# Two-bank PSUM tiles for attention scores and accumulators, and the two heads' score products issued in turn

## The chip, the cores and the metric

The kernel runs on one core of one Trainium2 chip. The core has a matrix engine (TensorE, PE in the profile) with its weight loads (PEld), VectorE (DVE), ScalarE (ACT), GpSimd (POOL) and SyncE (SP), which issues the transfers. PE writes its products to PSUM, here eight banks of 512 fp32 numbers for each of 128 partitions, and DVE and ACT read them from there. The metric is the device time of one execution in microseconds (us); less is better.

## The reference

Two layers of a decoder trunk on 256 tokens of width 1024, all in fp32. Each layer is a half SwiGLU feed-forward block (FFN, width 2816), a token mixer, and a second half FFN. Each block is normalised before and after.

```python
x = x + 0.5 * rms_norm(swiglu(rms_norm(x, g[0]), ...), g[1])
h = rms_norm(x, g[2])
m = pool_mixer(h, ...)  if i % 2 == 0 else  nsa_mixer(h, ...)
x = x + rms_norm(m, g[3])
x = x + 0.5 * rms_norm(swiglu(rms_norm(x, g[4]), ...), g[5])
```

The mixer of layer 0 pools: for each of four channel groups the mean over the last 2, 4, 8 or 16 tokens less the token itself, then a 256x256 product, a bias and a scale. The mixer of layer 1 is sparse attention with 16 heads of 64 numbers, 4 heads to a key group, and three branches: compressed blocks, selected blocks and a window. With 256 tokens the selected and the window branch each see all earlier tokens, so each is a causal softmax over the same mask but with keys and values of its own:

```python
s = jnp.einsum('bqgrd,btgd->bgrqt', qb, kb) * scale
p = jax.nn.softmax(jnp.where(mask, s, NEG_INF), axis=-1)
return jnp.einsum('bgrqt,btgd->bqgrd', p, vb)
```

## The kernel before

The tokens are two row tiles (t = 0, 1) of 128. An fp32 product is three matmuls on operands split into a high and a low part (mm3, L304 to L306; split and pieces_of make the parts, high on ACT, low on DVE, L294, L295, L309, L310). Weights arrive in pieces from HBM all through the program. The order of the instructions on each engine isn't written out: a scheduler, which simulates a timeline, chooses it, and Tile, the layer below, allots buffers from pools and puts in the waits. Both see a tile as one thing.

PSUM is two pools of four banks. psG holds short-lived products (tiles named g). psA has four one-bank tiles named acc, and acc_tiles hands out two of them, one for each half of 512 columns. These are the accumulators of an FFN's down products for a row tile (down), of the pooling stage's group product (pool_gemm) and its pooled output (pooled), of the attention output, and the score tiles of attention.

An accumulated pair goes through finish, which calls post: rstd squares both halves on ACT (L336, tile junk, with the sum into ssq), DVE adds the sums (L339, ms), POOL takes the power -0.5 (L341, rs), DVE multiplies each half by a gain (L348, into fx) and adds it to x (L350). For the next block emit then scales the row (L356, L357, L393) and transposes it on PE (L364, tile g). In the pooling stage group copies the two halves of the group product to pyh (ACT, L589) and pyl (DVE, L590), and pooled multiplies them by band matrices (L602).

Attention scores are made by qk(t, g). For each of two head pairs (pr) it fills one unit: two heads (par = 0, 1), whose queries and keys stand on partitions 0 to 63 and 64 to 127. Each head's scores for both branches are 256 columns for t = 0 and 512 for t = 1: three products (L837, operands kT and q), one product that adds the mask (L839, identr with amaskr), a maximum on DVE (L841, tile ast), and an exponential with its sum for each branch on ACT (L843, to fx or big). With two row tiles, four groups and two pairs there are 16 units, 8 of 256 and 8 of 512 columns, between 666 and 737 us. Later pv transposes the weights on PE (L881), splits them (PTh on ACT, PTl on DVE), and multiplies by the values (L862). The loop in qk is written so that the heads' products follow each other by twos, but each head has a tile of its own, and the scheduler is free to take one head's four products before the other's.

Of the kernel before, what the change touches and what calls it, by code (L numbers as in the profile page):

```python
# [9 lines left out]
F32 = mybir.dt.float32  # L10
# [5 lines left out]
PSUM = bass.MemoryType.PSUM  # L16

P = 128
# [218 lines left out]
def _trunk(ctx: ExitStack, tc: tile.TileContext, d, out):  # L237
    nc = tc.nc
    pp = ctx.enter_context(tc.tile_pool(name="pp", bufs=1))
    wp = ctx.enter_context(tc.tile_pool(name="wp", bufs=3))  # L240
    psA = ctx.enter_context(tc.tile_pool(name="psA", bufs=4, space=PSUM))
    psG = ctx.enter_context(tc.tile_pool(name="psG", bufs=4, space=PSUM))

    x = [pp.tile([P, DM], F32, name=f"x{t}") for t in range(NT)]
# [77 lines left out]
        return [v[:, H[h]] for h in range(2)]  # L322

    def acc_tiles():
        r = []
        for _ in range(2):
            acc = psA.tile([P, 512], F32, name="acc")
            r.append(acc)
        return r

    def rstd(src, half, t):
        s = pp.tile([P, 2], F32, name=f"ssq{t}", bufs=2)
# [76 lines left out]
    def ffn(i, j, pre, g_post, nxt, W0, preload, me=None):  # L409
        wg, wu, wd = d[f"wg{i}{j}"], d[f"wu{i}{j}"], d[f"wd{i}{j}"]  # L410
        with tc.tile_pool(name="fp", bufs=2, reuse_waits="tile") as fp:
# [8 lines left out]
            with ExitStack() if first else after(pre.h[0]):  # L420
                U = [W0[2], ksplit(piece(wu[:, 2048:4096], fp, "d", ND, 512), 8)]
            acc = [acc_tiles() for t in range(NT)]
            A = lambda t, k: [q[:, k, t * P:(t + 1) * P] for q in xT]
            hT, WD = {}, {}
# [146 lines left out]
    def pool_gemm(t, pre, W):  # L571
        acc = acc_tiles()
        xT = pre.at(t)
        for g in range(4):
            for k in range(2):
                m = mm3(acc[g // 2][:, g % 2 * 256:(g % 2 + 1) * 256], [q[:, 2 * g + k, :] for q in xT], W[2 * g + k], k == 0, k == 1)
        return acc, m

    def pool_mixer(pre, g_post, nxt, W0, preload, prep):
        with tc.tile_pool(name="mp", bufs=1, reuse_waits="tile") as mp:  # L580
# [12 lines left out]
            def pooled(t):  # L593
                o = acc_tiles()
                for g in range(4):
                    sl = slice(g * 256, (g + 1) * 256)
                    mm = [(sel[:, g, :], bias[q]) for q in range(2)]
                    mm += [(band[:, (t + b) * 4 + g, :], ys[b][q][:, sl]) for b in range(t + 1) for q in range(2)]
                    if t == 0:
                        mm.append((blo[:, g, :], ys[0][0][:, sl]))  # L600
                    for n, (A, B) in enumerate(mm):
                        nc.tensor.matmul(o[g // 2][:, g % 2 * 256:(g % 2 + 1) * 256], A, B, start=n == 0, stop=n == len(mm) - 1)  # L602
                return o
# [28 lines left out]
    def nsa(pre, g_post, nxt, W0, preload):  # L632
        with tc.tile_pool(name="np", bufs=1, reuse_waits="tile") as np_:
            identr = np_.tile([P, P], F32R, name="identr")
            amaskr = np_.tile([P, P], F32R, name="amaskr")
# [180 lines left out]
            def qk(t, g):  # L816
                nk = P * (t + 1)
                q = qT[g // 2, t]
                PP[t, g] = []
                for pr in range(2):  # L820
                    st = np_.tile([P, 2, 4], F32, name="ast", bufs=4)
                    pk_ = 2 * (g % 2) + pr
                    if pr == 0:
                        pe = fx[g % 2]
                    else:
                        pe = np_.tile([P, DM], F32, name="big", bufs=2)
                    pe = pe.rearrange("p (a k) -> p a k", a=4)
                    os_, mm = [], []
                    for par in range(2):
                        sp = psA.tile([P, 512], F32, name="acc")  # L830
                        o = sp[:, :2 * nk].rearrange("p (b k) -> p b k", b=2)
                        rs = slice(par * 64, (par + 1) * 64)
                        os_.append(o)
                        mm.append(([v[rs, pk_, :] for v in q], [v[rs, g, :, :nk] for v in kT]))
                    for i, j in ((0, 0), (0, 1), (1, 0)):
                        for o, (A, B) in zip(os_, mm):
                            nc.tensor.matmul(o, A[i], B[j], start=i + j == 0, stop=False)  # L837
                    for par, o in enumerate(os_):
                        nc.tensor.matmul(o[:, :, nk - P:], identr, amaskr[:, None, :].to_broadcast([P, 2, P]), start=False, stop=True)  # L839
                        i = par * 2  # L840
                        nc.vector.tensor_reduce(st[:, 0, i:i + 2], o, axis=AX.X, op=OP.max, negate=True)  # L841
                        for b in range(2):
                            nc.scalar.activation(pe[:, par * 2 + b, :nk], o[:, b, :], AF.Exp, bias=st[:, 0, i + b:i + b + 1],  # L843
                                                 accum_out=st[:, 1, i + b:i + b + 1])
                    yield
                    PP[t, g].append(pe)
                    r = np_.tile([P, 4], F32, name="ar", bufs=4)
                    nc.vector.reciprocal(r, st[:, 1])
                    gv = gates[t][:, 16:48].rearrange("p (b h) -> p h b", b=2)[:, 4 * g + 2 * pr:4 * g + 2 * pr + 2, :]
                    rv = r.rearrange("p (a b) -> p a b", b=2)  # L850
                    nc.vector.tensor_mul(rv, rv, gv)
                    nc.gpsimd.tensor_tensor(pe[:, :, :nk], pe[:, :, :nk], r[:, :, None].to_broadcast([P, 4, nk]), op=OP.mult)
                    yield
# [63 lines left out]
            qs, qn, ec, hm, wc, wo, acc = {}, {}, {}, {}, {}, [], []  # L917
# [17 lines left out]
            def step(kind, i, j):  # L935
                if kind in ("qk", "pv"):
                    if (kind, i, j) not in gens:
                        gens[kind, i, j] = {"qk": qk, "pv": pv}[kind](i, j)
# [57 lines left out]
    for c, hs, ls in ((0, [], pre[0].s), (1, [], pre[0].s), (2, pre[0].h[0], pre[0].h[0]), (3, pre[0].h[0], pre[0].h[0])):  # L996
        v = [q[:, c * 512:(c + 1) * 512] for q in W[0]]
        r = raw[c // 2][:, c % 2 * 512:(c % 2 + 1) * 512]
# [29 lines left out]
```

## Time and profile before

| | |
|---|---|
| median of 3 runs | 962.27 us (962.24 to 967.14) |
| profiled execution, span from first to last instruction | 963.9 us |
| mean granted PE clock | 0.993 of full speed |
| PE busy | 947.9 us, 98% |
| DVE, ACT, POOL busy | 581.1, 473.1, 82.2 us |

The profile is one execution; of its time only the span is recorded, and what lies around it is not. All times of rows are counted from the span's start. A row of a timeline gives the start, the busy time, engine, line, operation, written tile and read tiles with their shapes (partitions x elements), and how many like instructions it joins; in brackets stands the idle time before it and what ended it. PE's matmuls overlap, so their busy times add up to more than the time that passes: the price of a group is read from its start to the start of the next work.

### The profile page before, as it was taken

The page shows a single profiled execution, that of the slowest core. Times are in us where ns is not written, and L with a number is a line of the kernel's source. Part 1 is how long each engine was busy: PE and PEld are TensorE (multiplying, and loading weights), DVE is VectorE, ACT ScalarE, POOL GpSimd, SP SyncE. Part 2 cuts the span into 40 slices and gives each one's busy share as a digit, 9 for nine tenths or more (in the row PEclk, how much of TensorE's full clock was granted, in tenths as well). Part 3 has the DMA queues.
Part 4 walks back from the last instruction along what each step waited for, and adds up shares of the span by engine and source line. Part 5 has one row for each costly group of instructions (what it writes and reads, how often), then busy time and mean ns, then how long its engine had stood idle before and what let it go on. Part 6 is the DMA issues. An engine that isn't in the chain of part 4 may idle for free.

```text
span 963.9 us, 15935 instructions
## 1 busy us (share of the span) xinstructions
PE 947.9 (98%) x6418; PEld 861.8 (89%) x6418; DVE 581.1 (60%) x833; ACT 473.1 (49%) x812; POOL 82.2 (9%) x78
## 2 busy tenths in 40 slices
PE   8999999999999999999999999999999999999997
PEld 6999999989999999899999998888677799999996
DVE  5755554586854555567554456677986867554532
ACT  6744444355644444446443443545765655444421
POOL 1000000231000000120000001001455110000000
PEclk9999999999999999999999999999999899999999
DMA  8866666334866656248655652672200358666511
GB/s 302 280 219 235 209 190 191 101 129 136 291 230 201 191 176 218 89 144 293 216 180 186 203 177 68 256 260 90 88 1 5 122 194 295 203 197 180 184 45 44
DMA packets 47467, 169.14 MB, mean 175 GB/s; under 512 B 5529, under 2 KB 6041, under 8 KB 46882
## 3 DMA queue, kind: packets, MB, share of 16 engines
q1 hardware_dynamic: 47394, 168.13, 53.5%
q8 instruction: 50, 0.82, 0.4%
q14 instruction: 23, 0.19, 0.1%
HBM read 167.06 MB, written 1.05 MB: 174 GB/s over the span
## 4 chain that ended last, share of the span: by engine, by line
PE 91%; DVE 4%; ACT 2%; DMA 1%; issue 1%; POOL 1%; SPq 0%; DVEq 0%; POOLq 0%; ACTq 0%
PE g L306 18%; PE g L305 18%; PE g L304 18%; PE acc L306 9%; PE acc L304 9%; PE acc L305 9%; PE g L457 2%; PE acc L837 1%; PE g L862 1%; DVE wlo L295 1%; PE g L881 1%; PE g L364 1%; PE acc L602 1%; PE acc L839 1%; ACT whi L294 1%
## 5 line engine op out<-in xcount | busy, mean ns | idle before, releaser
L306 PE MATMUL g<-xTh,wlo 128*128 128x256 f32 x1152 | 327.8, 285 | 0.0
L305 PE MATMUL g<-xTl,whi 128*128 128x256 f32 x1152 | 326.8, 284 | 0.0
L304 PE MATMUL g<-xTh,whi 128*128 128x256 f32 x1152 | 324.5, 282 | 0.0
L295 DVE TENSOR_TENSOR wlo<-raw,whi 128x1024 fp32r<-128x1024 f32 (+2 forms) x252 | 244.4, 1012 | 94.0 <-ACT whi L294 93.4
L294 ACT ACTIVATE whi<-raw 128x1024 fp32r<-128x1024 f32 (+2 forms) x252 | 204.5, 862 | 184.2 <-issue 67.2
L304 PEld LDWEIGHTS g<-xTh,whi 128*128 128x128 f32 x1152 | 218.5, 190 | 1.2
L305 PEld LDWEIGHTS g<-xTl,whi 128*128 128x128 f32 x1152 | 216.7, 188 | 1.2
L306 PEld LDWEIGHTS g<-xTh,wlo 128*128 128x128 f32 x1152 | 217.6, 189 | 0.0
L295 DVE TENSOR_TENSOR dlo<-raw,dhi 128x1024 fp32r<-128x1024 f32 (+1 forms) x128 | 119.4, 956 | 120.0 <-ACT dhi L294 119.6
L294 ACT ACTIVATE dhi<-raw 128x1024 fp32r<-128x1024 f32 (+1 forms) x128 | 104.3, 843 | 143.3 <-DMA raw<-in_wd 137.0
L305 PE MATMUL acc<-dlo,hTh 128*128 128x512 f32 x288 | 112.6, 391 | 0.0
L304 PE MATMUL acc<-dhi,hTh 128*128 128x512 f32 x288 | 112.4, 390 | 0.0
L306 PE MATMUL acc<-dhi,hTl 128*128 128x512 f32 x288 | 112.1, 391 | 0.0
L429 DVE TENSOR_TENSOR sg<-sg,g 128x512 f32<-128x512 f32 x44 | 30.1, 685 | 92.3 <-PE g L306 92.3
L304 PE MATMUL g<-whi,xTh 128*128 128x256 f32 (+2 forms) x240 | 76.7, 322 | 1.9 <-ACT xTh L309 1.0
L306 PE MATMUL g<-whi,xTl 128*128 128x256 f32 (+2 forms) x240 | 76.6, 321 | 0.2
L305 PE MATMUL g<-wlo,xTh 128*128 128x256 f32 (+2 forms) x240 | 76.1, 319 | 0.0
L341 POOL TENSOR_TENSOR rs<-ms,neghalf 128x1 f32<-128x1 f32 x24 | 13.2, 548 | 611.5 <-DVE ms L339 611.5
L306 PEld LDWEIGHTS acc<-dhi,hTl 128*128 128x128 f32 x288 | 54.0, 188 | 11.5
L305 PEld LDWEIGHTS acc<-dlo,hTh 128*128 128x128 f32 x288 | 54.1, 188 | 10.6
L304 PEld LDWEIGHTS acc<-dhi,hTh 128*128 128x128 f32 x288 | 54.2, 188 | 10.4
L304 PEld LDWEIGHTS g<-whi,xTh 128*128 128x128 f32 x240 | 46.5, 194 | 5.7 <-ACT xTh L309 2.2
(194 smaller groups left out, 1137.5 us busy)
## 6 DMA issues: line engine op xcount, KB each, us to landing
raw<-in_wu SPq DMA_DIRECT2D x88, 512.0 KB, 4.6
raw<-in_wd SPq DMA_DIRECT2D x88, 512.0 KB, 4.6
raw<-in_wg SPq DMA_DIRECT2D x86, 512.0 KB, 4.2
raw<-in_win SPq DMA_DIRECT2D x18, 512.0 KB, 4.0
gain<-in_gains SPq DMA_DIRECT2D x11, 512.0 KB, 3.7
raw<-in_wo SPq DMA_DIRECT2D x8, 512.0 KB, 4.5
raw<-in_win SPq DMA_DIRECT2D x4, 304.0 KB, 2.9
raw<-in_wg SPq DMA_DIRECT2D x4, 256.0 KB, 4.6
```

What stands on the lines that cost most here:

```text
L294: nc.scalar.activation(hi[:, n + a:n + b], r[:, a:b], AF.Copy)
L295: nc.vector.tensor_tensor(lo[:, n + a:n + b], r[:, a:b], hi[:, n + a:n + b].bitcast(F32), op=OP.subtract)
L304: nc.tensor.matmul(o, A[0], B[0], start=start, stop=False)
L305: nc.tensor.matmul(o, A[0], B[1], start=False, stop=False)
L306: return nc.tensor.matmul(o, A[1], B[0], start=False, stop=stop)
L341: nc.gpsimd.tensor_tensor(r, v, neghalf, op=OP.pow)
L364: i = nc.tensor.transpose(pt[:, k, :], src[:, (4 * h + k) * P:(4 * h + k + 1) * P], ident)
L429: nc.vector.tensor_mul(sg, sg, pu)
L457: nc.tensor.matmul(o[:, u * 256:(u + 1) * 256], A(t, k)[i], B[u][k][j], start=n == 0, stop=n == len(its) - 1, skip_group_check=True)
L602: nc.tensor.matmul(o[g // 2][:, g % 2 * 256:(g % 2 + 1) * 256], A, B, start=n == 0, stop=n == len(mm) - 1)
L837: nc.tensor.matmul(o, A[i], B[j], start=i + j == 0, stop=False)
L839: nc.tensor.matmul(o[:, :, nk - P:], identr, amaskr[:, None, :].to_broadcast([P, 2, P]), start=False, stop=True)
```

## The change

psA has two tiles of two banks each instead of four of one bank: the same memory. acc_tiles returns the two halves of one such tile. In qk a unit takes its two score banks from one acc_tiles call, and the two mask products are issued behind all six score products, ahead of the maxima.

```diff
--- before.py
+++ after.py
@@ -238,7 +238,7 @@
     nc = tc.nc
     pp = ctx.enter_context(tc.tile_pool(name="pp", bufs=1))
     wp = ctx.enter_context(tc.tile_pool(name="wp", bufs=3))
-    psA = ctx.enter_context(tc.tile_pool(name="psA", bufs=4, space=PSUM))
+    psA = ctx.enter_context(tc.tile_pool(name="psA", bufs=2, space=PSUM))
     psG = ctx.enter_context(tc.tile_pool(name="psG", bufs=4, space=PSUM))
 
     x = [pp.tile([P, DM], F32, name=f"x{t}") for t in range(NT)]
@@ -322,11 +322,8 @@
         return [v[:, H[h]] for h in range(2)]
 
     def acc_tiles():
-        r = []
-        for _ in range(2):
-            acc = psA.tile([P, 512], F32, name="acc")
-            r.append(acc)
-        return r
+        acc = psA.tile([P, 2, 512], F32, name="acc")
+        return [acc[:, h] for h in range(2)]
 
     def rstd(src, half, t):
         s = pp.tile([P, 2], F32, name=f"ssq{t}", bufs=2)
@@ -826,17 +823,18 @@
                         pe = np_.tile([P, DM], F32, name="big", bufs=2)
                     pe = pe.rearrange("p (a k) -> p a k", a=4)
                     os_, mm = [], []
+                    sp = acc_tiles()
                     for par in range(2):
-                        sp = psA.tile([P, 512], F32, name="acc")
-                        o = sp[:, :2 * nk].rearrange("p (b k) -> p b k", b=2)
+                        o = sp[par][:, :2 * nk].rearrange("p (b k) -> p b k", b=2)
                         rs = slice(par * 64, (par + 1) * 64)
                         os_.append(o)
                         mm.append(([v[rs, pk_, :] for v in q], [v[rs, g, :, :nk] for v in kT]))
                     for i, j in ((0, 0), (0, 1), (1, 0)):
                         for o, (A, B) in zip(os_, mm):
                             nc.tensor.matmul(o, A[i], B[j], start=i + j == 0, stop=False)
+                    for o in os_:
+                        nc.tensor.matmul(o[:, :, nk - P:], identr, amaskr[:, None, :].to_broadcast([P, 2, P]), start=False, stop=True)
                     for par, o in enumerate(os_):
-                        nc.tensor.matmul(o[:, :, nk - P:], identr, amaskr[:, None, :].to_broadcast([P, 2, P]), start=False, stop=True)
                         i = par * 2
                         nc.vector.tensor_reduce(st[:, 0, i:i + 2], o, axis=AX.X, op=OP.max, negate=True)
                         for b in range(2):
```

Line numbers of the changed kernel are three lower behind acc_tiles (L837 is L834, L839 is L836 and L841 is L839 there, L843 is L841, L348 is L345).

On PE, where the third unit of 512 columns is multiplied (tiles acc, keys kT, queries q, transposes of fx by csm), there stands in the order of before:

```order
L862 MATMUL g_6917<-PTh_6918,VC0_6076 128x512 [waits Pool_49]
L862 MATMUL g_6917<-PTl_6919,VC0_6076 128x512 [waits Pool_49]
L837 MATMUL acc_7053<-kTh_6062,qh01_6765 128x512 [waits DVE_49,Activation_49]
L837 MATMUL acc_7053<-kTl_6063,qh01_6765 128x512
L837 MATMUL acc_7053<-kTh_6062,ql01_6766 128x512
L839 MATMUL acc_7053<-amaskr_6059,identr_6058 128x2x128
L837 MATMUL acc_7054<-kTh_6062,qh01_6765 128x512 [waits DVE_49,Activation_49]
L837 MATMUL acc_7054<-kTl_6063,qh01_6765 128x512
L837 MATMUL acc_7054<-kTh_6062,ql01_6766 128x512
L839 MATMUL acc_7054<-amaskr_6059,identr_6058 128x2x128
L881 MATMUL g_6928<-csm_74,fx0_69 128x128 [waits Activation_49,Pool_49]
```

and in that of after:

```order
L879 MATMUL g_6913<-csm_74,fx0_69 128x128 [waits DVE_49,Pool_49]
L879 MATMUL g_6913<-csm_74,fx0_69 128x128
L879 MATMUL g_6924<-csm_74,fx0_69 128x128 [waits Activation_49]
L879 MATMUL g_6924<-csm_74,fx0_69 128x128
L834 MATMUL acc_6959<-kTh_6051,qh01_6754 128x512 [waits DVE_49,Activation_49]
L834 MATMUL acc_6959<-kTh_6051,qh01_6754 128x512
L834 MATMUL acc_6959<-kTl_6052,qh01_6754 128x512 x2
L834 MATMUL acc_6959<-kTh_6051,ql01_6755 128x512 x2
L836 MATMUL acc_6959<-amaskr_6048,identr_6047 128x2x128 x2
L787 MATMUL g_6943<-kbd_6064,y_6822 128x32 [waits DVE_49]
L787 MATMUL g_6943<-kbd_6064,y_6822 128x32 x3
```

The two heads' products, one head whole after the other before, are now by twos in one tile, and two transposes each of the tiles behind have moved ahead of them. Only the unit's first product carries a wait in the new order.

On DVE, in the middle of the scores, with the maxima of two small units (ast from acc), there stands before:

```order
L841 TENSOR_REDUCE ast_7218<-acc_7219 128x2 [waits PE_49]
L851 TENSOR_TENSOR ar_7123<-ar_7123,gates1_6061 128x4 [waits DVE_49]
L841 TENSOR_REDUCE ast_7218<-acc_7220 128x2 [waits PE_49]
L310 TENSOR_TENSOR VC1_6077<-g_7026,VC1_6077 128x64 [waits Activation_49]
L310 TENSOR_TENSOR xTh_6950<-of_6952,xTh_6950 128x256 [waits Activation_49]
L841 TENSOR_REDUCE ast_7264<-acc_7266 128x2 [waits PE_49]
L848 RECIPROCAL ar_7188<-ast_7170 128x4 [waits Activation_49]
L899 TENSOR_TENSOR of_7020<-g_6990,y_7019 64x256 [waits DVE_49,Activation_49]
L899 TENSOR_TENSOR of_7020<-g_6990,y_7019 64x256
L851 TENSOR_TENSOR ar_7188<-ar_7188,gates1_6061 128x4 [waits DVE_49]
L310 TENSOR_TENSOR Pcl_7044<-g_7041,Pch_7043 128x128 [waits Activation_49]
L841 TENSOR_REDUCE ast_7264<-acc_7267 128x2 [waits PE_49]
```

and after, where the same two units are acc_7200 and acc_7246 (the first maximum of acc_7200 stands eight rows further up):

```order
L839 TENSOR_REDUCE ast_7244<-acc_7246 128x2 [waits PE_49]
L310 TENSOR_TENSOR PTl_7073<-g_7067,PTh_7072 128x512 [waits Activation_49,Pool_49]
L839 TENSOR_REDUCE ast_7199<-acc_7200 128x2 [waits Activation_49]
L310 TENSOR_TENSOR PTl_7084<-g_7078,PTh_7083 128x512 [waits PE_49,Activation_49]
L839 TENSOR_REDUCE ast_7244<-acc_7246 128x2 [waits Activation_49]
L310 TENSOR_TENSOR PTl_7115<-g_7109,PTh_7114 128x512 [waits PE_49,Activation_49]
L846 RECIPROCAL ar_7229<-ast_7199 128x4 [waits Activation_49]
```

Each maximum waited for PE; now the second of a unit waits for ACT. The second maximum of the first of these units stands behind the first maximum of the next one.

On DVE at the end of the kernel, where the first row tile of the last FFN is finished, there stands before:

```order
L348 TENSOR_TENSOR fx0_69<-acc_7897,gain_8026 128x512 [waits Activation_49]
L339 TENSOR_SCALAR ms0_9624<-ssq0_9619 128x1 [waits Activation_49]
L348 TENSOR_TENSOR fx0_69<-acc_7898,gain_8026 128x512
L350 SCALAR_TENSOR_TENSOR x0_67<-fx0_69,rs0_9626,x0_67 128x512 [waits Pool_49]
L350 SCALAR_TENSOR_TENSOR x0_67<-fx0_69,rs0_9626,x0_67 128x512 [waits DVE_49]
```

and after, from one row ahead:

```order
L310 TENSOR_TENSOR hTl_9561<-sg_9557,hTh_9560 128x512 [waits Activation_49]
L336 TENSOR_SCALAR ms0_9593<-ssq0_9588 128x1 [waits Activation_49]
L345 TENSOR_TENSOR fx0_69<-acc_7868,gain_7995 128x512 x2
L347 SCALAR_TENSOR_TENSOR x0_67<-fx0_69,rs0_9595,x0_67 128x512 [waits DVE_49,Pool_49]
L347 SCALAR_TENSOR_TENSOR x0_67<-fx0_69,rs0_9595,x0_67 128x512 [waits DVE_49]
```

The multiplication of half 0 stood ahead of ms and now stands behind it, with that of half 1.

## Rows read from the trace of the kernel before

**Rows 1.** The page: engines' busy time, share, instructions; chain that ended last, by engine.
```profile
PE 947.9 (98%) x6418; PEld 861.8 (89%) x6418; DVE 581.1 (60%) x833; ACT 473.1 (49%) x812; POOL 82.2 (9%) x78
...
PE 91%; DVE 4%; ACT 2%; DMA 1%; issue 1%; POOL 1%; SPq 0%; DVEq 0%; POOLq 0%; ACTq 0%
```

**Rows 2.** Windows: length, then busy us (instructions) of PE, PEld, DVE, ACT, POOL; PEclk.
```profile
666.00:696.00 30.00, 28.98 (x161) 20.78 (x160) 28.17 (x75) 23.10 (x81) 12.14 (x11) 1.00 0.21 71
696.00:726.00 30.00, 29.75 (x145) 20.92 (x145) 25.61 (x63) 21.11 (x78) 17.20 (x15) 0.94 0.00 1
726.00:750.00 24.00, 24.00 (x115) 18.96 (x114) 14.64 (x30) 12.84 (x34) 11.30 (x8) 1.00 0.11 28
```

**Rows 3.** A PE idle in PE's timeline, and the window behind it.
```profile
695.89 0.49 PE L862 MATMUL g<-PTl,V 128*128 128x512 f32 x1 [0.98 <-DVE PTl L310]
...
698.00:703.00 5.00, 5.00 (x20) 3.60 (x19) 4.96 (x14) 2.96 (x12) 1.93 (x2) 0.66 0.00 0
```

**Rows 4.** PE's timeline (start, us), score products of two heads in turn.
```profile
667.22 0.39 PE L837 MATMUL acc<-kTh,qh 64*128 64x256 f32 x2
...
668.21 0.39 PE L837 MATMUL acc<-kTh,qh 64*128 64x256 f32 x2
...
680.18 0.50 PE L837 MATMUL acc<-kTh,qh 64*128 64x512 f32 x2
...
681.62 0.66 PE L772 MATMUL g<-csm,y 128*128 128x128 f32 x4
```

**Rows 5.** PE's timeline, score products head after head.
```profile
670.98 0.39 PE L837 MATMUL acc<-kTh,qh 64*128 64x256 f32 x1
...
672.62 0.39 PE L304 MATMUL g<-whi,xTh 128*128 128x512 f32 x1
...
683.11 0.50 PE L837 MATMUL acc<-kTh,qh 64*128 64x512 f32 x1
...
685.43 0.38 PE L881 MATMUL g<-csm,fx 128*128 128x128 f32 x2
```

**Rows 6.** Groups by line and form, 666 to 726 us: reduces over scores.
```profile
L841 DVE TENSOR_REDUCE ast<-acc 128x2 f32<-128x512 f32 x14 | 9.4, 682 | 1.0 <-PE acc L839 0.8
...
L841 DVE TENSOR_REDUCE ast<-acc 128x2 f32<-128x256 f32 x16 | 6.4, 417 | 1.5 <-PE acc L839 1.5
```

**Rows 7.** ACT's timeline, two exps of a small and of a large unit.
```profile
681.62 0.37 ACT L843 ACTIVATE big<-acc,ast 128x128 f32<-128x128 f32 x1
...
681.96 0.38 ACT L843 ACTIVATE big<-acc,ast 128x128 f32<-128x128 f32 x1
...
685.73 0.48 ACT L843 ACTIVATE fx<-acc,ast 128x256 f32<-128x256 f32 x1 [1.63 <-PE g L881]
...
686.20 0.46 ACT L843 ACTIVATE fx<-acc,ast 128x256 f32<-128x256 f32 x1
```

**Rows 8.** ACT's and DVE's timelines at the end of the kernel.
```profile
956.24 0.60 ACT L336 ACTIVATE junk<-acc 128x512 bf16<-128x512 f32 x1 [8.83 <-PE acc L306]
...
957.60 0.60 ACT L336 ACTIVATE junk<-acc 128x512 bf16<-128x512 f32 x1 [0.67 <-PE acc L306]
...
959.26 1.41 DVE L350 SCALAR_TENSOR_TENSOR x<-fx,rs,x 128x512 f32<-128x512 f32 x2
```

**Rows 9.** DVE's and PE's timelines in the pooling stage.
```profile
207.69 0.74 DVE L590 SCALAR_TENSOR_TENSOR pyl<-acc,rs,pyh 128x512 fp32r<-128x512 f32 x1
...
212.69 1.42 DVE L350 SCALAR_TENSOR_TENSOR x<-fx,rs,x 128x512 f32<-128x512 f32 x2
...
218.03 1.03 PE L364 MATMUL g<-csm,fx 128*128 128x128 f32 x8
219.51 1.22 PE L457 MATMUL g<-whi,xTh 128*128 128x256 f32 x8 [0.45 <-ACT xTh L309]
```

**Rows 10.** DVE's and PE's timelines where the attention mixer's second output tile is transposed.
```profile
778.94 0.88 DVE L393 TENSOR_SCALAR fx<-fx,rs 128x512 f32<-128x512 f32 x2 [1.56 <-POOL rs L341]
...
779.69 0.71 PE L364 MATMUL g<-csm,fx 128*128 128x128 f32 x5
```

## The prediction

> **What bounds the kernel now.** I read the page first: its table of engines, then the chain that ended last [rows 1]. TensorE (PE) is busy 947.9 of 963.9 us and carries 91% of the chain. Work taken off PE is therefore a gain wherever nothing else takes its place, and a wait put before PE's next work is a loss. The edit touches scores in one stretch of the program only, the attention mixer at 666 to 750 us, so I read the busy time of every engine there by stages [rows 2]. The reader is to see two different stages. In 666 to 696 us VectorE (DVE) is busy 28.17 of 30 us and PE 28.98: both are full, and a slice of PE work saved there only makes PE wait for DVE sooner. In 696 to 726 us DVE has 25.61 of 30, so 4.4 us of air, and in 726 to 750 us PE is busy the whole 24 us with DVE at 14.64. Here PE sets the end. One PE wait inside this stretch is dear: after an idle of 0.98 us for a DVE operation the granted clock fell, and 698 to 703 us ran at a mean of 0.66, which is 0.34 x 5 = 1.7 us of PE lost behind the wait itself [rows 3].
>
> **What the change takes off PE.** There are 16 units (one row tile, one group, one pair of heads). The order before shows that in 4 of them the two heads' products already went in turn, and in 12 one head came whole after the other; in the order of after, all 16 go in turn. Both forms are in the trace of before, so the price needs no model. In turn, a 256-column unit takes 668.21 - 667.22 = 0.99 us to the next work, and a 512-column unit 681.62 - 680.18 = 1.44 us [rows 4]; a pair of equal matmuls costs the time of one, since the two heads stand in different halves of the array. Head after head, the 256-column unit takes 672.62 - 670.98 = 1.64 us and the 512-column unit 685.43 - 683.11 = 2.32 us [rows 5]. So 0.65 us is saved for each of 5 small units and 0.88 us for each of 7 large ones: 3.3 + 6.1 = 9.4 us of PE work. By place, one small and three large units lie before 696 us (0.65 + 2.65 = 3.3) and four of each after it (2.6 + 3.5 = 6.1).
>
> **What it adds behind the scores.** The order shows more than the diff does: waits now go by the two-bank tile. Before, the two heads' maxima (TENSOR_REDUCE) each waited for PE alone. Now the second waits for ScalarE (ACT), that is for the first head's two exponentials. A unit's evacuation becomes one file: reduce, two exps, reduce, two exps. The reduces take 0.68 us in a large unit and 0.42 in a small one [rows 6], and the exps follow each other at a pitch of 0.47 and 0.34 us [rows 7]. So a head takes 0.68 + 2 x 0.47 = 1.6 us or 0.42 + 2 x 0.34 = 1.1 us, and the pair 3.2 or 2.2 us; with the hand-overs between DVE and ACT I take 3.6 and 2.6. Before, the second reduce lay under the first head's exps. The tile comes free for PE only after the fourth exp, and there are two tiles instead of four. Queued behind a waiting reduce on DVE are the PTl splits that the next value products need, and PE waits for those.
>
> I walked the units along the printed order with these durations. The first unit that finds no free tile is the one that began at 683.11: both tiles are held by units whose exps ACT ends, one file after another, at about 683.5, so it moves little, and PE waits some 2 us ahead of it. The unit that began at 691.97 and the one at 696.70 then come out 0.7 us earlier or less: the 3.3 us of the first stage are eaten nearly whole. Of the later 6.1 the walk keeps more: the unit of 714.08 begins at about 711.45, 2.6 us ahead, and is itself 0.9 shorter. For the last three large units (2.6 us) I count nothing, because each finds a tile still held by exps. The mixer thus gains 2.6 + 0.9 = **3.5 us**. The bounds: 9.4 gained if every saving lands; nothing gained, or a loss (below), if DVE's new waits take it all.
>
> **What it adds elsewhere.** The accumulators of the feed-forward (FFN) and pooling stages use the same tiles, so a consumer of the first half now waits for the matmuls of the second.
>
> The end of the kernel is uncovered. Before, the square of half 0 ran at 956.24, under PE's last matmuls, and that of half 1 at 957.60; the two additions to x began at 959.26 [rows 8]. After, the first square starts where the second did, the second one square (0.70 us) later at 958.3, the mean at 959.1. Both multiplications, which follow it now, end at about 960.6, and then x. That is 960.65 - 959.26 = **+1.4 us**; 0.7 is the floor (the second square alone).
>
> The pooling stage is a chain of such steps on two row tiles, with PE's work around it short. In the new order pyh, pyl, pyh, pyl of the two halves are one file too. The DVE operation pyl of half 1 at 207.69 moves to about 209.2 (the FFN's x before it +1.3, then ACT's pyh between the two pyl). The addition to x at 212.69 moves to 214.95, 0.7 more for one square, and the transposes at 218.03 (PE waits 0.45 us behind them at 219.51) to about 219.95 [rows 9]: 1.95 us. The second row tile's later transposes add one square less what PE still has to do, 0.6 by estimate: **+2.6 us** in all; 0 if PE work can be pulled into the gap, 3.5 if nothing covers.
>
> The attention mixer's second output tile is exact as well: the normalised row is ready at 778.94 + 0.88 and its transposes start at 779.69 [rows 10], so a square more is **+0.7 us** (0 to 1.4). The other FFN ends have PE work beside them (one row tile's last products run while the other is normalised), and I price them at nothing; were that cover gone, each would be 0.7 to 1.4 us.
>
> **A rule that speaks against it.** The Trainium skill, in "TensorEngine Tiling (Array Packing)", section PSUM Bottleneck, says that packing the array speeds TensorE up and the evacuation of PSUM not at all, so that the evacuation may become the limit. The DVE column of the first stage agrees with that; it is the third rival below, not a term of the sum. The same skill's "PSUM — Partial Sum Buffer", section on bank collisions, asks that two engines be kept apart by bank, which would leave the two heads' banks free for DVE and ACT at once; the order shows that the program waits by tile all the same, and by that page alone the reduces would cost nothing and the sum be nearer the full gain.
>
> **Sum.** -3.5 + 1.4 + 2.6 + 0.7 = +1.2 us on the profiled execution's span of 963.9, so 965.1. That execution is 1.6 us above the median of the runs, 962.27 us; on the median I forecast 963.5. A measurement of this kernel can tell about 0.5% (4.8 us) from no change, and the runs of before spread over about as much.
>
> **Rivals.**
> 1. *The savings land.* If ACT and DVE drain the tiles before PE comes back, all 9.4 us leave the mixer: 1.2 - 5.9 = -4.7, 957.6 us; with the 0.66 clock of 698 to 703 spared as well, 955.9. For it: 6.1 of the 9.4 lie where DVE has air [rows 2], and DVE executes no more work than before. Against: two tiles, and 28.17 of 30 us before 696.
> 2. *The half-tile waits are hidden.* Then pooling and the mixer's output cost nothing and only the tail is left: -3.5 + 1.4 = -2.1, 960.2 us. For it: the FFN stages have work to move. Against: the 0.45 us that PE already waits at 219.51.
> 3. *DVE's head of queue, slower.* DVE takes its work in order, so a second reduce that waits for two exps (0.7 to 0.9 us) stops all behind it wherever no other operation was put between. Before 696 us there are 8 units: 8 x 0.8 = 6.4 us of new waits against 1.8 us of air, +4.6, and of the later 6.1 about 3 still lands: +1.6 in the mixer in place of -3.5, so +6.3 in all, 968.6 us. It decides from the point where the waits at the second reduces exceed about 5 us before 696. For it: the order puts between none and some fifteen operations between the two reduces of a unit. Against: in several units there is a PTl or other work between. A PE wait of some 2 us at 683 that brings the low clock once more (1.7 us) lies on its side.
> That the heads might not overlap is excluded by rows 4, and that the order is not changed by the order itself.
>
> **How the numbers follow.** The forecast's case, with each term within its bounds (960.5 to 967), has 0.50; the hidden waits 0.13; the savings that land 0.14; the slower case 0.23. The range 957 to 969 holds the first two and about half of each of the other two. Below 957.5 lies most of rival 1, since it spares some clock too (0.12), above 967.1 rival 3 and a little of the forecast's upper end (0.25), the rest between (0.63).
>
> **What would show it.** Every unit's score matmuls stand as pairs, 0.9 to 1.0 and 1.44 us a unit: if not, the 9.4 us are wrong. PE shows waits for ACT or DVE ahead of score products near 681 to 684 us, and DVE shows idle time put down to ACT ahead of the second reduces; if neither is there, rival 1 holds. The stretch from 666 us to the output transposes (now 779.69) shortens by about 3, the transposes of 218.03 come about 2 us later, and the last x 1.4 us later counted from the last matmul. The prediction is wrong by sign of the mixer if the stretch does not shorten, and by size if the pooling stage stays where it is.

## The result and the profile after

The changed kernel takes 980.83 us (980.03 to 981.88, 4 runs) against 964.7 us for the kernel before (962.24 to 967.26, 4 runs): a ratio of 1.0158, 95% interval 1.0129 to 1.0187: slower by 1.6%, clear of the noise. The profiled execution spans 977.9 us, 14.0 more than the 963.9 of before. (With more runs the median of before, 962.27 us when the forecast was made, came out between 964.7 and 966.5.)

From the page of the changed kernel: the engines, the granted PE clock in tenths over 40 slices of 24.4 us each, and the chain that ended last (beside [rows 1]). The last line is the clock over the 40 slices of the kernel before.

```profile
PE 947.2 (97%) x6418; PEld 858.7 (88%) x6418; DVE 579.2 (59%) x833; ACT 473.4 (48%) x812; POOL 78.3 (8%) x78
...
PEclk9999999978999999999999999999999899999999
...
PE 87%; DVE 6%; ACT 4%; issue 1%; DMA 1%; POOL 0%; SPq 0%; DVEq 0%; ACTq 0%; POOLq 0%
...
PEclk9999999999999999999999999999999899999999
```

PE is busy as long as before, though it was given 9.4 us less to do in the scores: something stretched it elsewhere. The clock row says where to look. It is below 9 in the ninth and tenth slices, 195.6 to 244.5 us, and that is the pooling stage. The 8 in the 32nd slice stands in the row of before as well.

The transposes of the normalised rows (L361, L364 before) stand at the same places of both programs, so they cut the time into stages. Here they are in the changed kernel's PE timeline.

```profile
199.16 1.05 PE L361 MATMUL g<-csm,fx 128*128 128x128 f32 x6
240.89 1.03 PE L361 MATMUL g<-csm,fx 128*128 128x128 f32 x8
416.60 1.03 PE L361 MATMUL g<-csm,fx 128*128 128x128 f32 x8
431.75 1.04 PE L361 MATMUL g<-csm,fx 128*128 128x128 f32 x8
607.30 1.03 PE L361 MATMUL g<-csm,fx 128*128 128x128 f32 x8
619.35 1.04 PE L361 MATMUL g<-csm,fx 128*128 128x128 f32 x8
776.15 0.60 PE L361 MATMUL g<-csm,fx 128*128 128x128 f32 x4
791.92 1.06 PE L361 MATMUL g<-csm,fx 128*128 128x128 f32 x8 [0.56 <-DVE fx L390]
```

The same rows of before stand at 198.94, 231.01, 406.04, 419.87, 595.33, 606.90, 764.63 and 779.69 us. That gives the length of each stage:

| stage, between transposes | before | after | difference |
|---|---|---|---|
| start and first FFN | 198.94 | 199.16 | +0.22 |
| pooling | 32.07 | 41.73 | **+9.66** |
| second FFN (to 419.87, 431.75) | 188.86 | 190.86 | +2.00 |
| third FFN (to 606.90, 619.35) | 187.03 | 187.60 | +0.57 |
| attention mixer | 157.73 | 156.80 | -0.93 |
| its second output tile | 15.06 | 15.77 | +0.71 |
| last FFN and end | 184.21 | 185.98 | +1.77 |

A row of transposes can come later without any loss, when PE does other work ahead of it. So it is between the two row tiles' transposes at the end of the second FFN, in the kernel before (first line) and the changed one:

```profile
406.04:419.87 13.83, 13.83 (x106) 13.32 (x105) 8.13 (x15) 6.59 (x15) 5.13 (x3) 1.00 0.42 137
416.60:431.75 15.15, 15.15 (x117) 14.65 (x116) 9.11 (x15) 6.36 (x15) 2.77 (x3) 1.00 0.39 136
```

PE is busy throughout at full clock in both; the 1.32 us more are 11 more products of 0.12 us, which the third FFN then no longer has to do. At the end of the third FFN 4 products (0.48 us) moved in the same way. Counted with the same work, the second FFN is 2.00 - 1.32 = 0.68 us longer, the third 0.57 + 1.32 - 0.48 = 1.41 us, and the mixer is -0.93 + 0.48 = 0.45 us shorter. The first row of the table is uncertain: the kernels below with one-bank accumulators reach these transposes at 197.2 to 197.6 us and those with two-bank ones at 199.2 to 199.6, so the first FFN may have lost more than 0.22 us.

**The pooling stage** holds two thirds of the loss. First PE's timeline where it begins to go wrong (in brackets the idle time before the row and what ended it), then the windows of the stage, with the whole stage of before as the last line (length, busy us of PE, PEld, DVE, ACT, POOL, then the granted clock).

```profile
207.18 0.39 PE L599 MATMUL acc<-pyh,band 128*128 128x256 f32 x1 [0.51 <-ACT pyh L586]
208.63 0.66 PE L361 MATMUL g<-csm,fx 128*128 128x128 f32 x4 [1.06 <-POOL fx L353]
209.04 0.39 PE L599 MATMUL acc<-pyl,band 128*128 128x256 f32 x1
209.24 0.40 PE L599 MATMUL acc<-pyh,blo 128*128 128x256 f32 x1
209.57 0.58 PE L599 MATMUL acc<-biash,sel 4*128 4x256 f32 x1
```

```profile
200.00:209.00 9.00, 7.32 (x46) 6.22 (x45) 5.60 (x9) 4.95 (x12) 2.61 (x3) 1.00 0.16 59
209.00:220.00 11.00, 11.00 (x48) 9.53 (x46) 5.02 (x10) 2.63 (x7) 1.99 (x3) 0.53 0.15 49
220.00:223.00 3.00, 2.60 (x13) 1.79 (x12) 1.71 (x4) 2.60 (x6) 1.13 (x2) 0.98 0.00 0
223.00:230.00 7.00, 6.67 (x27) 5.36 (x27) 2.77 (x7) 2.78 (x8) 0.73 (x2) 0.52 0.00 0
...
198.94:231.01 32.07, 31.57 (x224) 28.24 (x225) 25.82 (x45) 18.89 (x43) 8.83 (x10) 1.00 0.32 100
```

PE waits 0.51 us for pyh, which now waits for the whole group product, and 1.06 us for the row that the FFN's late end delays. At 209.2 the clock goes to the lower of its two levels, 1.2 GHz in place of 2.4: the same bias product takes 0.58 us instead of 0.38. It stays there to 219.4, rises, and falls once more behind a wait of 0.40 us. The means of 0.53 over 11 us and 0.52 over 7 us are 0.47 x 11 + 0.48 x 7 = 8.5 us of PE's work that had to be done later. In the kernel before the clock was 1.00 throughout this stage, although PE waited there too, 0.45 us at 219.51 [rows 9].

**The attention mixer** did what was written for it. Two units of the changed kernel that go straight on to other work, one of each size, from PE's timeline:

```profile
680.88 0.39 PE L834 MATMUL acc<-kTh,qh 64*128 64x256 f32 x2
...
681.87 0.39 PE L834 MATMUL acc<-kTh,qh 64*128 64x256 f32 x2
...
706.87 0.50 PE L834 MATMUL acc<-kTh,qh 64*128 64x512 f32 x2
...
708.27 0.50 PE L860 MATMUL g<-PTl,VC 128*128 128x512 f32 x1
```

They take 0.99 and 1.40 us, against 0.99 and 1.44 in [rows 4]. But PE now waits, as these rows of the list of PE's waits from 660 to 790 us show (total us, times, longest).

```profile
PE g L860 <- DVE PTl L310: 3.0, 6, 1.1
PE acc L834 <- ACT fx L841: 1.3, 2, 0.9
PE g L860 <- DVE cst L798: 1.2, 1, 1.2
...
PE g L879 <- ACT big L841: 0.9, 1, 0.9
PE g L879 <- DVE Pcl L310: 0.8, 1, 0.8
PE acc L834 <- ACT big L841: 0.7, 1, 0.7
```

Between the first unit and the last one's evacuation the timeline shows 8.9 us of idle PE in 15 waits, against 1.2 us in two waits before. The mixer's row of the table also holds 1.98 us that are not its own. At its head ACT's queue held the split of the second row tile's transposes behind a copy (L675) that waited for DVE, as before, and now behind one more copy (L685), which used to follow the split:

```profile
620.28 1.06 ACT L675 ACTIVATE fx<-y 128x1024 f32<-128x1024 f32 x1 [2.74 <-DVE y L666]
621.24 0.58 ACT L685 ACTIVATE y<-g 128x512 f32<-128x512 f32 x1
621.72 1.08 ACT L309 ACTIVATE xTh<-g 128x512 fp32r<-128x512 f32 x2
...
622.36 0.50 PE L304 MATMUL g<-whi,xTh 128*128 128x512 f32 x1 [1.98 <-ACT xTh L309]
```

The row that they transpose was late because both squares came after the third FFN's last product. Without that wait, and with the same work, the mixer is 0.45 + 1.98 = 2.4 us shorter than before.

Part of this is the clock. Before, a spell at 698 to 703 us cost 1.7 us [rows 3], and the changed kernel's profile has none among its scores. Both have one at the end of the mixer (first line before, second after):

```profile
756.50:763.20 6.70, 6.14 (x16) 4.66 (x17) 4.13 (x10) 2.23 (x6) 0.55 (x1) 0.52 0.01 2
768.50:775.70 7.20, 6.23 (x14) 4.30 (x15) 5.54 (x12) 2.65 (x8) 1.26 (x2) 0.54 0.02 6
```

**The end**, against [rows 8] (PE, ACT and DVE timelines):

```profile
970.06 0.39 PE L306 MATMUL acc<-dhi,hTl 128*128 128x512 f32 x1
...
970.54 0.60 ACT L333 ACTIVATE junk<-acc 128x512 bf16<-128x512 f32 x1 [9.53 <-PE acc L306]
...
971.26 0.60 ACT L333 ACTIVATE junk<-acc 128x512 bf16<-128x512 f32 x1
...
973.31 1.40 DVE L347 SCALAR_TENSOR_TENSOR x<-fx,rs,x 128x512 f32<-128x512 f32 x2
```

Both squares stand behind the last product, and x begins 973.31 - 970.06 = 3.25 us after it. Before, the last product began at 957.12 us and x at 959.26, 2.14 us later. So the tail grew by 1.11 us.

### The profile page after: what moved, and what is told of

It reads as the page before. It is cut to its first block, busy times and chain, and to the rows that moved or that the text cites. A ratio compares the mean times of both kernels' runs of the same rounds, so it can differ in the third digit from the quotient of the medians.

```text
span 977.9 us, 15929 instructions
## 1 busy us (share of the span) xinstructions
PE 947.2 (97%) x6418; PEld 858.7 (88%) x6418; DVE 579.2 (59%) x833; ACT 473.4 (48%) x812; POOL 78.3 (8%) x78
## 4 chain that ended last, share of the span: by engine, by line
PE 87%; DVE 6%; ACT 4%; issue 1%; DMA 1%; POOL 0%; SPq 0%; DVEq 0%; ACTq 0%; POOLq 0%
PE g L306 18%; PE g L305 18%; PE g L304 18%; PE acc L306 9%; PE acc L304 9%; PE acc L305 9%; PE g L454 1%; PE acc L599 1%; DVE wlo L295 1%; ACT junk L333 1%; PE g L361 1%; PE g L860 1%; DMA x<-in_x 1%; DVE ast L839 1%; DVE x L347 1%
## 5 line engine op out<-in xcount | busy, mean ns | idle before, releaser
L295 DVE TENSOR_TENSOR wlo<-raw,whi 128x1024 fp32r<-128x1024 f32 (+2 forms) x252 | 241.8, 1003 | 91.1 <-ACT whi L294 90.4
```

The costliest lines, as they stand in the source:

```text
L295: nc.vector.tensor_tensor(lo[:, n + a:n + b], r[:, a:b], hi[:, n + a:n + b].bitcast(F32), op=OP.subtract)
```

## The experiments

Theory A: the loss sits in the accumulators outside the mixer, and most of it is the half clock that follows short PE waits in the pooling stage; the mixer gains a little. Its rival B: the loss is the mixer's second reduces, which wait for ACT (the third rival of the prediction), and the rest moves along. Ratios are to the kernel before in the same sitting, whose median was 965.45 us for the useless work and for the last experiment, and 966.54 for the four others.

**The change in the mixer only.** A pool of two-bank tiles is opened for the attention mixer and one of one-bank tiles before and after it.

```diff
+    psum(False)   # acc_tiles: two one-bank tiles
     pre[0].g = acc_tiles()
...
+    psum(True)    # acc_tiles: one two-bank tile
     W = nsa(pre[4], 9, pre[5], W, pre_ffn(1, 1))
+    psum(False)
     ffn(1, 1, pre[5], 11, None, W, None)
```

> Two-bank tiles and products in turn inside the attention mixer only; the feed-forward and pooling stages get four one-bank tiles as before. Theory A (the loss lies in the accumulators outside the mixer): the pooling stage goes back to its old length (9.7 us), the feed-forward ends too (1.3 and 2.5 us), the mixer keeps its gain of 2.6 us and its output tile's 1.0 us of loss: 962.3 - 2.6 + 1.0 = 960.7 us, 959 to 962. Theory B (the loss is the scores' second reduces that wait for ACT, and what lies ahead of the mixer moves only along with it): slower than before, 970 or more.

Measured: 964.11 us, ratio 0.9988 (0.9963 to 1.0013), the same as before. The pooling stage takes 32.05 us and the second and third FFN 188.87 and 187.03, as before within 0.02: the losses are gone, so B falls. The mixer, though, takes 158.90 us and not 155, and the time is above the range that theory A gave. The clock shows why:

```profile
674.00:682.30 8.30, 5.48 (x40) 3.66 (x38) 8.05 (x22) 6.68 (x22) 0.00 (x0) 0.98 0.68 223
682.30:693.00 10.70, 10.70 (x42) 7.57 (x44) 7.84 (x21) 6.07 (x24) 4.80 (x4) 0.54 0.06 24
```

In the changed kernel the same piece of program, with the same four waits (0.73, 0.80, 0.55 and 0.74 to 0.75 us), kept its clock:

```profile
690.00:698.00 8.00, 5.25 (x37) 3.48 (x35) 7.76 (x21) 6.59 (x22) 0.00 (x0) 1.00 0.68 214
698.00:710.00 12.00, 10.73 (x65) 7.42 (x65) 10.27 (x28) 9.02 (x34) 7.83 (x6) 1.00 0.08 34
```

So up to 0.46 x 10.7 = 4.9 us of the mixer's time hang on whether such a spell comes, and the runs of this kernel spread from 961.57 to 968.87.

**The change everywhere but in the mixer**, with the score units of before:

```diff
     psum(True)    # two-bank accumulators
...
+    psum(False)   # one-bank tiles, scores as before
     W = nsa(pre[4], 9, pre[5], W, pre_ffn(1, 1))
+    psum(True)
```

> The other half of the change alone: one-bank tiles in the attention mixer with the heads' products as the scheduler orders them, two-bank accumulators in the feed-forward and pooling stages. Theory A: all of the loss and none of the gain, 980.4 + 2.6 - 1.0 = 982 us, 980 to 984, with two spells of half clock, some 17 us, between 209 and 230 us. Theory B: about as before, 962 to 966.

Measured: 982.95 us, ratio 1.0179 (1.0137 to 1.0221). All of the loss without the scores' part. The pooling stage takes 41.81 us, with the two spells of half clock in their places:

```profile
209.50:220.00 10.50, 10.50 (x46) 9.23 (x44) 4.93 (x10) 2.57 (x6) 1.85 (x3) 0.53 0.16 51
223.00:230.40 7.40, 7.06 (x29) 5.86 (x30) 3.12 (x7) 3.26 (x9) 1.09 (x2) 0.55 0.00 0
```

Theory A holds for the place. Nor are the two spells a chance of one execution: the three profiles with the changed kernel's pooling stage (the changed kernel, this one and the one with the joint maximum below) all have both, and the four with one-bank tiles there have none.

**Useless work in the pooling stage's PE waits.** 16 more matmuls, whose result nobody reads, behind the bias products (6) and behind the first pyh product (10). All waits stay.

```diff
+            def fill(n):
+                z = psG.tile([P, 512], F32, name="g")
+                for k in range(n):
+                    nc.tensor.matmul(z[:, :256], band[:, 8, :], W[0][0], start=k == 0, stop=k == n - 1)
...
+                        if t == g == 0 and n in (1, 2):
+                            with after([i]):
+                                fill((6, 10)[n - 1])
```

> The changed kernel with 16 useless matmuls of 256 columns put on PE in the pooling stage: 6 behind the first bias products and 10 behind the first pyh product, where PE sat idle for 0.51 and 1.06 us. All waits stay. Theory A (the idle itself costs little and the half clock that follows it costs the rest): the spells of half clock of 10.2 and 6.8 us go, the stage loses 1 to 2 us in place of 9.7, and the time falls by 6 to 8 us: 972 to 975. Theory D (the stage is long because of the file of waits, and the clock only stretches PE where it waits anyhow): within 2 us of the changed kernel, 979 to 983.

Measured: 976.04 us, ratio 1.0127 (1.0094 to 1.0159), 4.8 us under the changed kernel's median: between the two theories. By the ratios the gain is only 0.3%, 3 us, and the intervals overlap, so the times alone don't prove it. The mean granted clock of the runs speaks for it: 0.989 to 0.993 in four of six (0.982 and 0.986 in the others), against 0.982 to 0.986 in all four runs of the changed kernel. The profile shows the rest. PE's timeline shows the added work where PE had been idle, and the windows the clock behind it.

```profile
206.82 0.98 PE L593 MATMUL g<-whi,band 128*128 128x256 f32 x6
207.64 0.28 PE L604 MATMUL acc<-pyh,band 128*128 128x256 f32 x1
207.76 1.36 PE L593 MATMUL g<-whi,band 128*128 128x256 f32 x10
208.96 0.60 PE L361 MATMUL g<-csm,fx 128*128 128x128 f32 x4
```

```profile
209.00:220.00 11.00, 9.88 (x64) 8.08 (x63) 7.81 (x15) 5.58 (x13) 3.30 (x4) 0.97 0.17 53
219.30:226.50 7.20, 7.20 (x31) 6.08 (x30) 3.00 (x7) 2.88 (x8) 1.09 (x2) 0.53 0.01 2
```

The first spell is gone, with more PE work and the same dependences; the second is not, and PE still waits ahead of it (0.24 and 0.88 us at 216.2 and 218.1). The stage falls from 41.73 to 37.61 us, which is the whole difference of the two profiles (977.9 and 973.7 us). What is left above before is 5.5 us, and 0.47 x 7.2 = 3.4 of it is the second spell. So by this sum the waits themselves, with the added work in them, cost the stage some 2 us, and the clock the rest. That the second spell would go with its waits was not tried.

**One maximum for both heads**, in the changed kernel:

```diff
+                    nc.vector.tensor_reduce(st[:, 0].rearrange("p (a b) -> p a b", a=2), acc[:, :, :2 * nk].rearrange("p a (b k) -> p a b k", b=2),
+                                            axis=AX.X, op=OP.max, negate=True)
                     for par, o in enumerate(os_):
                         i = par * 2
-                        nc.vector.tensor_reduce(st[:, 0, i:i + 2], o, axis=AX.X, op=OP.max, negate=True)
```

> The changed kernel with one maximum over both heads of a unit (one DVE instruction over both banks) in place of two. No DVE operation waits for exps any more; the four exps follow each other on ACT. Theory A1 (the mixer's PE waits come from the second reduces): 3 to 7 us under the changed kernel, 974 to 978. Theory A2 (they come from having two tiles that ACT frees late): within 2 us of the changed kernel, 979 to 982.

Measured: 973.78 us, ratio 1.0076 (1.0051 to 1.0102), 7 us under the changed kernel by the medians and 4.8 by the profiles (977.9 and 973.1 us). The mixer's stage falls from 156.80 to 151.94 us with PE idle for 4.6 us in 7 waits where it had been 8.9 in 15. A2 falls. But A1 is not right in its mechanism: DVE hardly stood still for the exps. In the changed kernel's list of DVE's waits from 676 to 750 us, the second reduces have only the first row below, and the last unit's adds the second, from DVE's timeline. That is 1.3 us in all; before, DVE waited 4.5 us for PE ahead of reduces.

```profile
DVE ast L839 <- ACT fx L841: 0.2, 1, 0.2
...
751.46 0.69 DVE L839 TENSOR_REDUCE ast<-acc 128x2 f32<-128x512 f32 x1 [1.09 <-ACT big L841]
```

In the other units the scheduler had put other work between. What the joint maximum shortens, as far as the order tells, is the file of a unit (reduce, exps, reduce, exps becomes reduce and four exps), and with it everything that waits for the fourth exp. How much of the 4.9 us is the file and how much the new order on ACT was not separated.

**The heads in turn with one-bank tiles**, in the kernel before:

```diff
-                    os_, mm = [], []
+                    os_, mm, mm_ = [], [], []
...
-                            nc.tensor.matmul(o, A[i], B[j], start=i + j == 0, stop=False)
+                            with after(mm_[-1:]):
+                                mm_.append(nc.tensor.matmul(o, A[i], B[j], start=i + j == 0, stop=False))
```

> The kernel before with one-bank tiles, only that each score product is made to issue behind the other head's product of the same round, so that the heads go in turn. Theory A (PE's saving is real and the two-bank tile's waits eat it): no reduce waits for ACT's exps, so most of the 9.4 us lands where PE sets the end: 954 to 959 us. Theory C (the mixer's evacuation on DVE and ACT eats the saving whatever the tiles are): 960 to 963.

Measured: 959.1 us, ratio 0.9926 (0.9898 to 0.9954), faster, by 7 us. The mixer's stage takes 152.68 us, 5.0 less than before, though a spell of half clock cost it 0.43 x 12 = 5.2 us here (692 to 704 us), about as much as the two of before (1.7 and 0.48 x 6.7 = 3.2). In five units other products stand between the two heads' first ones. More than half of the 9.4 us lands all the same, and theory C falls: PE's saving is real, and in the changed kernel the tile that spans two banks, with a maximum for each head, took most of it back.

**Two-bank tiles in the mixer only, with the joint maximum**: the first experiment's edit and the fourth's.

> Two-bank tiles inside the attention mixer only, with one maximum over both heads of a unit. The pooling and feed-forward stages are those of before. The joint maximum took 7 us off the changed kernel's mixer, on top of nothing lost outside: 962.3 - 6.8 + 1.0 = 956.5 us, 954 to 960, about as the one-bank tiles in turn (959.1). If the mixer's gain hangs on where its clock spells fall: up to 965.

Measured: 956.73 us, ratio 0.9917 (0.9891 to 0.9942): the best kernel of the study, with the one-bank version level with it within the intervals. The mixer's stage takes 149.90 us, 7.8 less than before, of which some 1.5 us is less half clock (3.4 us lost against 4.9), and the two-bank tile's cost at its output, 770.64 - 754.87 = 15.77 us against 15.06, is still paid. One DVE row shows what it gained besides: the joint maximum of a large unit takes 1.22 us where two took 2 x 0.68.

```profile
679.96 1.22 DVE L852 TENSOR_REDUCE ast<-acc 128x4 f32<-128x1024 f32 x1
```

## Why the prediction was wrong

It forecast no change, 963.5 us in 957 to 969, and the kernel took 980.83. By its own steps:

- **What the change takes off PE**: right. 15 of the 16 units go in turn whole, at the prices of [rows 4]; in the last one, at 746.90, four transposes stand between the two heads' first products. With one-bank tiles the heads in turn make the kernel 7 us faster, so the saving was real.
- **What it adds behind the scores**: right in kind, the waits too small, and the balance near the mark by luck. The mixer was to gain 3.5 us and gained some 2.4, and PE waits ahead of score products and of products that need PTl, as said. But the new waits took 8.9 - 1.2 = 7.7 us where the forecast had 9.4 - 3.5 = 5.9. That leaves 1.7 of the 9.4 us, half of what was forecast. The clock spell of before [rows 3], which the changed kernel's profile doesn't have there, adds another 1.7, and no term counted on it.
- **The pooling stage, +2.6 us: the step that failed.** It measured +9.66. The chain of late steps was seen rightly, and with the useless work in PE's waits about 2 us remain for it. What was left out is what a PE wait does to the clock. That price stood in the prediction, read from [rows 3] (0.98 us idle, then 0.34 x 5 us lost), but it was applied to the mixer alone. Here two sums of short waits, 0.51 + 1.06 and later 0.40 us, were followed by 10 and 7 us at half clock, 8.5 us of PE's work.
- **The other FFN ends, nothing: failed too.** Counted with the same work, they cost 0.68 us in the second FFN, 1.41 + 1.98 in the third, and 1.77 - 1.11 = 0.66 us in the last. The row tile that is normalised beside PE work was thought covered. In the third FFN its lateness let another copy in ahead of the transposes' split on ACT. The prediction gave 0.7 to 1.4 us for each such end if the cover was gone; that is about what the ends cost, but for the 1.98 us at the head of the mixer, which come on top.
- **The second output tile, +0.7**: measured +0.71. **The tail, +1.4**: measured +1.11.

Of the rivals, the third was forecast on the right side and for the wrong place: DVE's second reduces waited 1.3 us for ACT, where it had 6.4 us before 696 alone, and the kernel with only the accumulators changed is as slow without any of them. The sum of what was measured, 0.22 + 9.66 + 2.00 + 0.57 - 0.93 + 0.71 + 1.77, is 14.0 us, the difference of the spans.

The rule from the Trainium skill's "TensorEngine Tiling (Array Packing)", section PSUM Bottleneck, that packing doesn't speed the evacuation up, agrees with the mixer in part: PE's 9.4 us came back as waits of 7.7 us for the work on ACT and DVE. But with one-bank tiles and the same evacuation PE's idle time in the mixer's stage is 6.1 us, against 4.6 before and 14.6 in the changed kernel (12.6 without the wait at the stage's head), so most of these waits come with the tile. The loss of the kernel lies elsewhere.

## What to carry to other kernels

In this program a tile is the unit of waiting. Making one tile of two ties every reader of the first half to the writer of the second, in all places that share the pool: look at those ends first, and give the tile its new shape only in the stage that needs it, with reads that span it (one maximum for two heads). An order that is wanted can be asked for directly, without a shared tile. And where a wait is put in front of an engine that was never idle, price the clock behind it as well, in every stage where the wait is new.

## What the runs showed of the hardware

A PE wait of some tenths of a microsecond can be followed by many times its length at half clock: 0.51 and 1.06 us of idle PE by 10 us at 0.53, 0.40 us by 7 us at 0.52. The same instructions with the same waits do not always get it: 2.8 us of waits in four pieces were followed by 10.7 us at 0.54 in one kernel and by 12 us at 1.00 in another that issues the same work there. A wait of 1.98 us at 622.36 left the changed kernel's clock at 1.00 from 620 to 630 us; the same wait of 1.99 us in the kernel with the change everywhere but in the mixer was followed by a mean of 0.79 from 620 to 628. Work that nobody reads, put into two waits, kept the clock up behind them (0.97 over 11 us in place of 0.53) and shortened the stage by 4.1 us in the profile.
